# Loading a ring in single 2 MB units for three expert pairs, and a bias spread over five, in a one-core trunk kernel

## The chip, the core and the metric

The kernel runs on one core of a Trainium2 chip. The metric is device time in microseconds of one execution, the median of three runs. A profile of one further execution is at hand; its times are those of the trace.

## What is computed

One decoder layer on 256 tokens of width 1024, float32 throughout: an adaLN-conditioned token mixer (three branches, gated and projected), then an expert FFN, then a final RMSNorm. The part that matters here is the FFN. A router picks 4 of 32 experts for each token; an expert has a gate-up matrix of 1024 x 2048, a clamped SwiGLU, a down matrix of 1024 x 1024, and biases for both:

```python
def expert_block(args):
    xb, e = args
    gu = xb @ w_gu[e] + b_gu[e]
    gate, up = jnp.split(gu, 2, axis=-1)
    gate = jnp.minimum(gate, SWIGLU_LIMIT)
    up = jnp.clip(up, -SWIGLU_LIMIT, SWIGLU_LIMIT)
    glu = gate * jax.nn.sigmoid(SWIGLU_ALPHA * gate)
    return ((up + 1.0) * glu) @ w_down[e] + b_down[e]
...
y_assign = ys[dest] * w_sorted[:, None]
out = jax.ops.segment_sum(y_assign, sorted_tok, num_segments=n_tok)
```

All 32 experts' weights are read once from HBM: 403 MB of the 485 MB that the kernel moves.

## The kernel before

**Pairs.** The FFN goes through the experts in 16 pairs. For pair `p`, `gate_up(p)` multiplies the gathered tokens by eight blocks of 128 rows of both experts' gate-up matrices (`k` = 0 to 7, 2 MB each); after each block a function `during(k)` slips in other work: the gather of the next pair's tokens, block by block (`gather_k`, L1173), and after block 0 the scatter of an earlier pair's result (L1327). Then come `swiglu(p)` on VectorE and ScalarE and `down(p - 1)`, the down projections of the pair before, 4 MB for each of the two experts. So TensorE's order is gate-up 0, gate-up 1, down 0, gate-up 2, down 1 and so on. Both kinds of product are recorded at L1337 (`tiles4`); 32 of its passes belong to one gate-up block, 16 to one of the eight row blocks of a down projection.

**The ring.** Weights land in `wchunk`, a ring of seven units of 2 MB, with loads issued by SP in the order in which `add` put them on the list `loads`. `lay` assigns units: a load of size 1 takes the unit that was used longest ago, a load of size 2 an aligned couple (0 and 1, 2 and 3, or 4 and 5), so that unit 6 is left out where only such couples run. The turn of the single loads is laid so that the first couple falls on units 0 and 1. A load is issued as soon as TensorE has done the last matmul on what stood in its unit; SP waits for that, and all later loads wait behind it. A "wide" load (`add_gu2`, and a slot of size 2 in `add_dn`) is two DMAs of 2 MB, one for each expert, with rows of 16 KB, for two blocks `k`; a couple is given back by `passed` after the second of them.

**Exceptions.** `EXTRA` names blocks that are loaded singly (`add_gu`): (0, 6) in the ring, (0, 7) into free pieces of other tiles ("rest"), (1, 6) and (1, 7) into "b2" and "b4", which the mixer has left. Pair 15 and the last down projections are loaded in smaller slots; these don't change.

**The down bias.** The sum of the down biases over each token's experts is one product of the routing weights (transposed into `wT`) with the 32 rows of biases. `bias_down` does it whole, in `during(1)` of pair 7: two transposes (L1277), a copy by VectorE, and four products of 128 x 512 (L1282), each into one of the two banks of `bbank`, multiplied and added to the residual by VectorE (`add_rows`, L1268 and L1270).

Of the kernel before, what the change touches and what calls it, by code (L numbers as in the profile page):

```python
# [20 lines left out]
D = 1024  # L21
KB = D // P
T = 256
TT = T // P
FF = 1024
NE = 32
TOPK = 4
NP = NE // 2
HEADS = 8
EPS = 1e-5  # L30
SPILL = 12
LIMIT = 7.0
ALPHA = 1.702
# [43 lines left out]
def trunk(ctx: ExitStack, tc: tile.TileContext, x, c, norm1_g, ada_w, ada_b, w_in, gmlp_norm_g, gmlp_ws,  # L77
# [3 lines left out]
    V, S, G, TE = nc.vector, nc.scalar, nc.gpsimd, nc.tensor  # L81
# [28 lines left out]
    def bbank():  # L110
        return psb.tile([P, 512], F32, name="bbank")
# [8 lines left out]
    def add(fn, where=None, size=1):  # L120
        loads.append((fn, where, size))
        return len(loads) - 1
# [53 lines left out]
    def load(dst, src):  # L176
        nc.sync.dma_start(dst, src)  # L177
# [64 lines left out]
    wgu, wdn = exp_w_gu[0], exp_w_down[0]  # L242
    gu_ids, dn_ids = {}, {}


    EXTRA = {(0, KB - 2): None, (0, KB - 1): "rest", (1, KB - 2): "b2", (1, KB - 1): "b4"}

    def gu_rows(p, j):
        return wgu[2 * p:2 * p + 2, 2 * j * P:2 * (j + 1) * P, :].rearrange("e (p i) n -> p e i n", i=2)
# [11 lines left out]
    def add_gu(p, k):  # L261
        src = gu_rows(p, k // 2)[:, :, k % 2]

        def fn(t):
            c = 0
            for v in t if isinstance(t, list) else [t]:
                v = v.rearrange("p (e n) -> p e n", e=2)
                load(v, src[:, :, c:c + v.shape[2]])
                c += v.shape[2]
        gu_ids[p, k] = (add(fn, EXTRA[p, k]), None)  # L270

    def dn_rows(w, k0, k, c0, n):
        j, i = k0 // 4, k0 % 4
        v = w[4 * j * P:4 * (j + 1) * P]
        if (k, n) == (4, D):
            return v.rearrange("(p i) n -> p (i n)", i=4)
        return v[:, c0:c0 + n].rearrange("(p i) n -> p i n", i=4)[:, i:i + k]

    def add_dn(p, *slots):

        dn_ids[p] = []

        def fn(t, parts):
            off = 0
            for k0, k, c0, n in parts:
                for e in range(2):
                    v = t[:, off:off + k * n]
                    load(v if (k, n) == (4, D) else v.rearrange("p (k n) -> p k n", k=k), dn_rows(wdn[2 * p + e], k0, k, c0, n))
                    off += k * n
        for parts in slots:  # L290
            size = sum(2 * a[1] * a[3] for a in parts) // CHUNK_ELEMS
            i = add(lambda t, parts=parts: fn(t, parts), None, size)
            off = 0
            for a in parts:
                dn_ids[p].append((i, off, a is parts[-1]) + a)
                off += 2 * a[1] * a[3]

    for p in range(NP):
        for j in range(KB // 2):
            if (p, 2 * j) not in EXTRA:  # L300
                add_gu2(p, j)
            elif p == 0:
                for i in range(2):
                    add_gu(p, 2 * j + i)
            if (p, j) == (0, 1):
                for pk_ in EXTRA:
                    if pk_[0]:
                        add_gu(*pk_)
        if p:
            add_dn(p - 1, *([[(4 * j, 4, 0, D)] for j in range(2)] if p < NP - 1 else  # L310
                            [[(k, 4, c, 512)] for c in (0, 512) for k in (0, 4)]))
    add_dn(NP - 1, [(0, 4, 0, 512)], [(4, 2, 0, 512), (6, 2, 0, 512)], [(0, 4, 512, 256), (4, 4, 512, 256)],
           [(0, 4, 768, 256), (4, 2, 768, 256), (6, 2, 768, 256)])
# [25 lines left out]
    b4 = Carve(big.tile([P, CHUNK_ELEMS], F32, name="b4"))  # L339
# [92 lines left out]
    def half(h):  # L432
        return slice(h * 512, (h + 1) * 512)
# [555 lines left out]
    for o in order:  # L989
# [6 lines left out]
        name, h = o  # L996
# [38 lines left out]
    n = len(steps)  # L1035
# [94 lines left out]
    wk = {"g2b": big.tile([P, D], F32, name="x4", bufs=2)}  # L1130
# [134 lines left out]
    def add_rows(ps, tt, s, gate=False):  # L1265
        if gate:
            t = wk["su"]()
            V.tensor_tensor(t, ps, wk["g2b"][:, s], op=OP.mult)  # L1268
            ps = t
        V.tensor_tensor(xt[:, tt, s], ps, xt[:, tt, s], op=OP.add)  # L1270

    def bias_down():

        wT = wk["wT"]
        ps = bbank()
        for tt in range(TT):
            TE.transpose(ps[:NE, tt * P:(tt + 1) * P], wgt[:, tt], ident)  # L1277
        V.tensor_copy(wT, ps[:NE, :T].rearrange("p (t n) -> p t n", t=TT))
        for tt in range(TT):
            for h in range(2):  # L1280
                ps = bbank()
                TE.matmul(ps, lhsT=wT[:, tt], rhs=wk["bdn"][:, half(h)], start=True, stop=True)  # L1282
                add_rows(ps, tt, half(h), gate=True)

    def swiglu(pg, a=None):

# [69 lines left out]
    def gate_up(p, during=None):  # L1356
        sel[p] = nc.values_load(isel[0:1, p:p + 1], engines=[PE], min_val=0, max_val=1,
                                skip_runtime_bounds_check_because="one minus the result of a comparison: 0 or 1")
        pg = [abank() for _ in range(4)]
        for i, k in enumerate(in_turn(p)):  # L1360
            n, row = gu_ids[p, k]
            t = chunk(n)
            ws = []
            for v in t if isinstance(t, list) else [t]:
                v = v.rearrange("p (e n) -> p e n", e=2)
                if row is not None:
                    v = v[:, :, row * 2 * FF:(row + 1) * 2 * FF]
                ws.extend(v[:, :, c:c + 512] for c in range(0, v.shape[2], 512))
            for b in range(4):
                tiles4(pg[b], xs[p % 2][:, k], lambda e: of_expert(ws[b], e, slice(0, 512)), sel[p], i == 0, False)  # L1370
            if EXTRA.get((p, k)) is None and row != 0:
                passed(n)
            if during:
                during(i)
            if i == KB - 2:
                V.tensor_copy(ex.rearrange("p (a g) -> p a g", a=4), e2g[:, p].unsqueeze(2).to_broadcast([P, 4, GRP]))
        add_bias(pg)
        return pg
# [91 lines left out]
    for p in range(1, NP):  # L1470
        weigh(p - 1)
        if p > 1:
            turn_weights(p - 1)
            transpose_act()

        def during(k, p=p):
            if k == 0 and p >= 2:
                scatter(owT[p - 2])
            if k == 1 and p == 7:
                bias_down()  # L1480
            if p + 1 < NP:
                if k == 0:
                    one_hot(p + 1)
                else:
                    gather_k(p + 1, k - 1)
                if k == KB - 1:
                    gather_k(p + 1, k)
        pg = gate_up(p, during)
        if p == 1:
            more_work_tiles()  # L1490
            turn_weights(p - 1)
            transpose_act()
        swiglu(pg)
        if p == SPILL:
            tail = Carve(big.tile([P, CHUNK_ELEMS], F32, name="b2"))
            aT, scr1, scr2 = tail(FF).rearrange("p (k n) -> p k n", k=KB), tail(FF), tail(2 * FF)
            spills(scr2, scr1, xs[p % 2])
        if p < NP - 1:
            down(p - 1)


    p = NP - 1
# [68 lines left out]
```

## Time and profile before

| | |
|---|---|
| median of 3 runs | 1292.19 us (1291.4 to 1294.12) |
| the profiled execution | 1296.29 us |
| its span, first to last instruction | 1294.7 us |
| TensorE busy | 1217.2 us, 94% |
| VectorE, ScalarE busy | 439.9 us, 270.8 us |
| moved by DMA | 484.72 MB, 374 GB/s over the span |
| mean granted TensorE clock | 0.979 |

The mixer fills the first 340 us or so; the pairs begin at about 346. The profile cuts the span into 40 equal slices; a timeline tells what an engine ran when; the waits tell who ended an engine's idle time; and for some of the loads the trace has the time from issue to landing. A busy TensorE is not a TensorE at its peak, since matmuls are pipelined and their ends are modelled.

### The profile page before, as it was taken

What the parts mean: (1) busy time and instruction counts of PE and PEld (TensorE: products, weight loads), DVE (VectorE), ACT (ScalarE), POOL (GpSimd) and SP (SyncE); (2) the same over time, 40 slices, a digit from 0 to 9 for tenths busy, and PEclk for the clock granted to TensorE, in tenths of its full rate; (3) what the DMA queues carried; (4) which work ended last, traced back from release to release, by engine and by line L of the source; (5) the groups of instructions that cost most, each with busy time, mean ns of one, the idle gap of its engine ahead of it and who ended that gap; (6) DMA issues with size and microseconds to landing.
All of it is one profiled execution on the core that took longest, in us unless ns stands there. A gap on an engine that the chain in (4) does not pass through costs nothing. (4 is left out here: it accounts for less than half of the span.)

```text
span 1294.7 us, 22543 instructions
## 1 busy us (share of the span) xinstructions
PE 1217.2 (94%) x9653; PEld 614.1 (47%) x9654; DVE 439.9 (34%) x884; ACT 270.8 (21%) x538; POOL 11.0 (1%) x27
## 2 busy tenths in 40 slices
PE   7999999999899999898989899999989898989897
PEld 5899998999633333233333233333333333323222
DVE  3477886877431211212131223111121213121122
ACT  5564554455320000001010001000000101000011
POOL 0010000000000000000000000000000000000001
PEclk9999999999999999999999989999999999999999
DMA  9997198297798899999999989999999999999996
GB/s 342 322 386 256 49 381 296 104 390 311 258 390 360 351 427 427 427 428 428 426 426 427 427 358 429 427 426 426 427 427 427 427 427 425 420 421 427 427 389 224
DMA packets 83764, 484.72 MB, mean 374 GB/s; under 512 B 6753, under 2 KB 21161, under 8 KB 59854
## 3 DMA queue, kind: packets, MB, share of 16 engines
q1 hardware_dynamic: 82982, 481.51, 91.5%
q10 hardware_dynamic: 680, 1.71, 0.4%
q8 instruction: 80, 1.31, 0.4%
q14 instruction: 22, 0.18, 0.0%
HBM read 482.16 MB, written 1.05 MB: 373 GB/s over the span
## 5 line engine op out<-in xcount | busy, mean ns | idle before, releaser
L1337 PE MATMUL abank<-wchunk,b 128*32 (+2 forms) x4160 | 489.8, 608 | 34.9 <-DMA wchunk<-in_exp_w_down_dram 26.6
L1337 PEld LDWEIGHTS abank<-wchunk,b 128*32 128x32 f32 x4160 | 138.3, 112 | 342.4 <-issue 312.4
L1337 PE MATMUL cbank<-wchunk,b 128*32 128x512 f32 (+2 forms) x1952 | 232.5, 595 | 3.7 <-DMA wchunk<-in_exp_w_gu_dram 3.7
L1110 DVE TENSOR_SCALAR b<-bbank,a,mod 128x128 f32<-128x128 f32 x64 | 26.2, 410 | 395.9 <-PE bbank L1173 395.9
L509 DVE TENSOR_TENSOR spl<-wchunk,spl 128x512 fp32r<-128x512 f32 x196 | 132.2, 691 | 49.1 <-ACT spl L508 46.2
L1108 ACT ACTIVATE b<-bbank,mod,a 128x128 f32<-128x128 f32 x64 | 29.2, 457 | 537.9 <-PE bbank L1173 537.9
L508 ACT ACTIVATE spl<-wchunk 128x512 fp32r<-128x512 f32 x196 | 120.8, 627 | 76.3 <-PE abank L519 46.5
L516 PE MATMUL abank<-b,spl 128*128 128x256 f32 x432 | 110.3, 287 | 0.0
L1173 PEld LDWEIGHTS bbank<-spl,b 128*128 128x128 f32 x512 | 66.4, 193 | 91.4 <-issue 89.4
L517 PE MATMUL abank<-b,spl 128*128 128x256 f32 x432 | 108.3, 283 | 0.0
L1337 PEld LDWEIGHTS cbank<-wchunk,b 128*32 128x32 f32 x1952 | 55.0, 110 | 110.9 <-issue 98.1
L1173 PE MATMUL bbank<-spl,b 128*128 128x128 f32 x512 | 87.2, 300 | 1.8 <-DVE spl L1166 0.9
L516 PEld LDWEIGHTS abank<-b,spl 128*128 128x128 f32 x432 | 82.7, 191 | 3.6 <-issue 2.5
L517 PEld LDWEIGHTS abank<-b,spl 128*128 128x128 f32 x432 | 82.8, 192 | 0.2 <-issue 0.2
L1393 DVE TENSOR_TENSOR row<-abank,x 128x512 f32<-128x512 f32 (+1 forms) x32 | 21.8, 683 | 179.6 <-PE abank L1337 179.6
L1270 DVE TENSOR_TENSOR xt<-bbank,xt 128x512 f32<-128x512 f32 (+1 forms) x66 | 44.6, 675 | 107.6 <-PE bbank L1327 107.6
L519 PE MATMUL abank<-b,spl 128*128 128x256 f32 x432 | 69.7, 283 | 0.0
L1327 PE MATMUL bbank<-row,b 128*128 128x512 f32 (+1 forms) x132 | 62.7, 605 | 1.6 <-DVE row L1393 1.4
L519 PEld LDWEIGHTS abank<-b,spl 128*128 128x128 f32 x432 | 59.7, 192 | 0.0
L516 PE MATMUL cbank<-b,spl 128*128 128x256 f32 x224 | 57.2, 287 | 0.0
L517 PE MATMUL cbank<-b,spl 128*128 128x256 f32 x224 | 56.2, 283 | 0.0
L1320 ACT ACTIVATE b<-bbank 128x256 f32<-128x256 f32 x16 | 6.1, 383 | 238.5 <-PE bbank L1318 238.5
(273 smaller groups left out, 847.2 us busy)
## 6 DMA issues: line engine op xcount, KB each, us to landing
wchunk<-in_exp_w_gu_dram SPq DMA_DIRECT2D x125, 2048.0 KB, 17.3
wchunk<-in_exp_w_down_dram SPq DMA_DIRECT2D x56, 2048.0 KB, 14.6
wchunk<-in_w_in_dram SPq DMA_DIRECT2D x16, 2048.0 KB, 9.4
wchunk<-in_ada_w_dram SPq DMA_DIRECT2D x8, 2048.0 KB, 12.9
wchunk<-in_exp_w_down_dram SPq DMA_DIRECT2D x10, 1024.0 KB, 14.4
wchunk<-in_ada_w_dram SPq DMA_DIRECT2D x16, 512.0 KB, 9.5
wchunk<-in_exp_w_down_dram SPq DMA_DIRECT2D x10, 512.0 KB, 12.9
wchunk<-in_w_in_dram SPq DMA_DIRECT2D x4, 1024.0 KB, 10.5
```

Source lines behind the costliest of these rows:

```text
L508: S.activation(hi, w, AF.Copy)
L509: V.tensor_tensor(lo, w, hi.bitcast(F32), op=OP.subtract)
L516: TE.matmul(out_, lhsT=wh, rhs=xh, start=first and i == 0, stop=False)
L517: TE.matmul(out_, lhsT=wh, rhs=xl, start=False, stop=False)
L519: TE.matmul(out_, lhsT=wl, rhs=xh, start=False, stop=last_ and i == n - 1)
L1108: S.activation(out_, in_, AF.Identity, scale=a2[:, k:k + 1], bias=sh2[:, k:k + 1])
L1110: V.tensor_scalar(out_, in_, a2[:, k:k + 1], sh2[:, k:k + 1], op0=OP.mult, op1=OP.add)
L1173: TE.matmul(ps, lhsT=xn2[:, tt, k * P:(k + 1) * P], rhs=oh[p][:, tt].rearrange("p a g -> p (a g)"), start=tt == 0, stop=tt == TT - 1)
L1270: V.tensor_tensor(xt[:, tt, s], ps, xt[:, tt, s], op=OP.add)
L1327: TE.matmul(ps, lhsT=wt[:, tt * P:(tt + 1) * P], rhs=wk["yv"][:, c:c + n], start=True, stop=True)
L1337: TE.matmul(out_[g * GRP:(g + 1) * GRP], lhsT=xl[:, g * GRP:(g + 1) * GRP], rhs=w(e), start=start, stop=stop, skip_group_check=True)
L1393: V.tensor_tensor(wk["yv"][:, c:c + m], bank[c], wk["g2b"][:, c:c + m], op=OP.mult)
```

## The change

Two things. First, a constant `FINE` = 3: pairs 0 to 2 load each gate-up block singly, one DMA of 2 MB with rows of 8 KB, and the down projections of pairs 0 and 1 in four slots of one unit each (two row blocks of both experts, two DMAs of 1 MB). Wide loads begin with pair 3. (0, 6) is then no exception any more. Second, `bias_down` is cut: `turn_routing` does the transposes and the copy in pair 4, and one of the four products stands in each of pairs 5 to 8, at the same place behind the second block.

```diff
--- before.py
+++ after.py
@@ -28,6 +28,7 @@
 NP = NE // 2
 HEADS = 8
 EPS = 1e-5
+FINE = 3
 SPILL = 12
 LIMIT = 7.0
 ALPHA = 1.702
@@ -243,7 +244,7 @@
     gu_ids, dn_ids = {}, {}
 
 
-    EXTRA = {(0, KB - 2): None, (0, KB - 1): "rest", (1, KB - 2): "b2", (1, KB - 1): "b4"}
+    EXTRA = {(0, KB - 1): "rest", (1, KB - 2): "b2", (1, KB - 1): "b4"}
 
     def gu_rows(p, j):
         return wgu[2 * p:2 * p + 2, 2 * j * P:2 * (j + 1) * P, :].rearrange("e (p i) n -> p e i n", i=2)
@@ -267,13 +268,13 @@
                 v = v.rearrange("p (e n) -> p e n", e=2)
                 load(v, src[:, :, c:c + v.shape[2]])
                 c += v.shape[2]
-        gu_ids[p, k] = (add(fn, EXTRA[p, k]), None)
+        gu_ids[p, k] = (add(fn, EXTRA.get((p, k))), None)
 
     def dn_rows(w, k0, k, c0, n):
         j, i = k0 // 4, k0 % 4
         v = w[4 * j * P:4 * (j + 1) * P]
-        if (k, n) == (4, D):
-            return v.rearrange("(p i) n -> p (i n)", i=4)
+        if n == D:
+            return v.rearrange("(p i) n -> p (i n)", i=4)[:, i * D:(i + k) * D]
         return v[:, c0:c0 + n].rearrange("(p i) n -> p i n", i=4)[:, i:i + k]
 
     def add_dn(p, *slots):
@@ -285,7 +286,7 @@
             for k0, k, c0, n in parts:
                 for e in range(2):
                     v = t[:, off:off + k * n]
-                    load(v if (k, n) == (4, D) else v.rearrange("p (k n) -> p k n", k=k), dn_rows(wdn[2 * p + e], k0, k, c0, n))
+                    load(v if n == D else v.rearrange("p (k n) -> p k n", k=k), dn_rows(wdn[2 * p + e], k0, k, c0, n))
                     off += k * n
         for parts in slots:
             size = sum(2 * a[1] * a[3] for a in parts) // CHUNK_ELEMS
@@ -295,19 +296,22 @@
                 dn_ids[p].append((i, off, a is parts[-1]) + a)
                 off += 2 * a[1] * a[3]
 
+
     for p in range(NP):
         for j in range(KB // 2):
-            if (p, 2 * j) not in EXTRA:
+            if p < FINE:
+                for i in range(2):
+                    if p == 0 or (p, 2 * j + i) not in EXTRA:
+                        add_gu(p, 2 * j + i)
+            else:
                 add_gu2(p, j)
-            elif p == 0:
-                for i in range(2):
-                    add_gu(p, 2 * j + i)
             if (p, j) == (0, 1):
                 for pk_ in EXTRA:
                     if pk_[0]:
                         add_gu(*pk_)
         if p:
-            add_dn(p - 1, *([[(4 * j, 4, 0, D)] for j in range(2)] if p < NP - 1 else
+            add_dn(p - 1, *([[(4 * j, 4, 0, D)] for j in range(2)] if FINE <= p < NP - 1 else
+                            [[(2 * q, 2, 0, D)] for q in range(4)] if p < FINE else
                             [[(k, 4, c, 512)] for c in (0, 512) for k in (0, 4)]))
     add_dn(NP - 1, [(0, 4, 0, 512)], [(4, 2, 0, 512), (6, 2, 0, 512)], [(0, 4, 512, 256), (4, 4, 512, 256)],
            [(0, 4, 768, 256), (4, 2, 768, 256), (6, 2, 768, 256)])
@@ -1269,18 +1273,18 @@
             ps = t
         V.tensor_tensor(xt[:, tt, s], ps, xt[:, tt, s], op=OP.add)
 
-    def bias_down():
-
-        wT = wk["wT"]
+    def turn_routing():
+
         ps = bbank()
         for tt in range(TT):
             TE.transpose(ps[:NE, tt * P:(tt + 1) * P], wgt[:, tt], ident)
-        V.tensor_copy(wT, ps[:NE, :T].rearrange("p (t n) -> p t n", t=TT))
-        for tt in range(TT):
-            for h in range(2):
-                ps = bbank()
-                TE.matmul(ps, lhsT=wT[:, tt], rhs=wk["bdn"][:, half(h)], start=True, stop=True)
-                add_rows(ps, tt, half(h), gate=True)
+        V.tensor_copy(wk["wT"], ps[:NE, :T].rearrange("p (t n) -> p t n", t=TT))
+
+    def bias_down(tt, h):
+
+        ps = bbank()
+        TE.matmul(ps, lhsT=wk["wT"][:, tt], rhs=wk["bdn"][:, half(h)], start=True, stop=True)
+        add_rows(ps, tt, half(h), gate=True)
 
     def swiglu(pg, a=None):
 
@@ -1368,7 +1372,7 @@
                 ws.extend(v[:, :, c:c + 512] for c in range(0, v.shape[2], 512))
             for b in range(4):
                 tiles4(pg[b], xs[p % 2][:, k], lambda e: of_expert(ws[b], e, slice(0, 512)), sel[p], i == 0, False)
-            if EXTRA.get((p, k)) is None and row != 0:
+            if (p, k) not in EXTRA and row != 0:
                 passed(n)
             if during:
                 during(i)
@@ -1476,8 +1480,10 @@
         def during(k, p=p):
             if k == 0 and p >= 2:
                 scatter(owT[p - 2])
-            if k == 1 and p == 7:
-                bias_down()
+            if k == 1 and p == 4:
+                turn_routing()
+            if k == 1 and 5 <= p < 9:
+                bias_down(*divmod(p - 5, 2))
             if p + 1 < NP:
                 if k == 0:
                     one_hot(p + 1)
```

SP's loads from the first of the experts' on, before (`wchunk` is the ring, the `b` tiles are "b2", "b4" and a part of "rest", of which `spl` and `row` are the other parts; x4 is four DMAs alike):

```order
L177 DMA wchunk<-in_exp_w_gu_dram 128x4096 x4
L177 DMA b_3512<-in_exp_w_gu_dram 128x2x2048
L177 DMA b_3530<-in_exp_w_gu_dram 128x2x2048
L177 DMA wchunk<-in_exp_w_gu_dram 128x4096 x2
L177 DMA wchunk<-in_exp_w_gu_dram 128x2x2048
L177 DMA b_3798<-in_exp_w_gu_dram 128x2x1024
L177 DMA spl<-in_exp_w_gu_dram 128x2x512
L177 DMA row<-in_exp_w_gu_dram 128x2x512
L177 DMA wchunk<-in_exp_w_gu_dram 128x4096 x6
L177 DMA wchunk<-in_exp_w_down_dram 128x4096 x4
L177 DMA wchunk<-in_exp_w_gu_dram 128x4096 x8
L177 DMA wchunk<-in_exp_w_down_dram 128x4096 x4
```

and with the change:

```order
L178 DMA wchunk<-in_exp_w_gu_dram 128x2x2048 x4
L178 DMA b_3512<-in_exp_w_gu_dram 128x2x2048
L178 DMA b_3530<-in_exp_w_gu_dram 128x2x2048
L178 DMA wchunk<-in_exp_w_gu_dram 128x2x2048 x3
L178 DMA b_3798<-in_exp_w_gu_dram 128x2x1024
L178 DMA spl<-in_exp_w_gu_dram 128x2x512
L178 DMA row<-in_exp_w_gu_dram 128x2x512
L178 DMA wchunk<-in_exp_w_gu_dram 128x2x2048 x6
L178 DMA wchunk<-in_exp_w_down_dram 128x2048 x8
L178 DMA wchunk<-in_exp_w_gu_dram 128x2x2048 x8
L178 DMA wchunk<-in_exp_w_down_dram 128x2048 x8
L178 DMA wchunk<-in_exp_w_gu_dram 128x4096 x8
```

The order of the data is the same; the wide rows of 4096 elements up to the second down projection have become loads of 2 x 2048 and of 2048, and twice as many for the down projections.

TensorE in pair 7 behind the second block, before (`cbank` and `abank` are the banks of gate-up, `ident` the identity, the `b` tile of L1282 has the turned weights and the biases):

```order
L1337 ISA
L1337 MATMUL abank<-wchunk,b_3650 32x512 x4
L1277 MATMUL bbank<-ident,x_3753 32x128 x2
L1282 MATMUL bbank<-b_4281 128x512 x4
L1173 MATMUL bbank<-spl,b_3798 128x128 x2
L1337 ISA
L1337 MATMUL cbank<-wchunk,b_3650 32x512 x4
```

With the change, at that place in pair 4:

```order
L1341 ISA
L1341 MATMUL abank<-wchunk,b_3650 32x512 x4
L1280 MATMUL bbank<-ident,x_3753 32x128 x2
L1177 MATMUL bbank<-spl,b_3798 128x128 x2
L1341 ISA
L1341 MATMUL cbank<-wchunk,b_3650 32x512 x4
```

and in pair 5 (as in 6, 7 and 8):

```order
L1341 ISA
L1341 MATMUL abank<-wchunk,b_3650 32x512 x4
L1286 MATMUL bbank<-b_4286 128x512
L1177 MATMUL bbank<-spl,b_3798 128x128 x2
L1341 ISA
L1341 MATMUL cbank<-wchunk,b_3650 32x512 x4
```

The block of two transposes and four products stands in five pieces, each ahead of the gather of that block.

## Rows read from the trace of the kernel before

**Rows 1.** The page: the span, and the bytes moved in 40 equal slices of it.
```profile
span 1294.7 us, 22543 instructions
...
GB/s 342 322 386 256 49 381 296 104 390 311 258 390 360 351 427 427 427 428 428 426 426 427 427 358 429 427 426 426 427 427 427 427 427 425 420 421 427 427 389 224
```

**Rows 2.** Windows: stretch, length, busy us by engine, PEclk, DMA share, GB/s.
```profile
344.00:360.00 16.00, 15.07 (x116) 6.51 (x120) 3.41 (x6) 2.21 (x4) 0.00 (x0) 0.90 0.42 111
748.00:752.00 4.00, 4.00 (x20) 1.39 (x23) 1.75 (x4) 0.00 (x0) 0.00 (x0) 0.50 1.02 434
752.00:764.00 12.00, 12.00 (x100) 4.11 (x96) 0.41 (x1) 0.61 (x2) 0.00 (x0) 0.94 0.64 243
500.00:740.00 240.00, 221.16 (x1764) 77.94 (x1760) 46.93 (x85) 18.68 (x36) 0.00 (x0) 0.98 1.01 427
```

**Rows 3.** Waits of the DMA queue on SP: total us, times, longest.
```profile
SPq L177 <- PE abank L1337: 691.5, 77, 17.9
```

**Rows 4.** Timeline of SP: start, us, loads sent out after a wait.
```profile
356.06 0.82 SPq L177 DMA_DIRECT2D wchunk<-in_exp_w_gu_dram  x2
...
427.52 0.81 SPq L177 DMA_DIRECT2D wchunk<-in_exp_w_gu_dram  x2
...
502.89 0.80 SPq L177 DMA_DIRECT2D wchunk<-in_exp_w_gu_dram  x2
```

**Rows 5.** Two loads by tile: issue times, then us from issue to landing.
```profile
L177 SPq DMA_DIRECT2D wchunk<-in_exp_w_gu_dram x2: 328/377/426, 489.1 to 489.5; - x2
...
DMA to landing us min/median/max: 17.1/19.5/22.0
...
L177 SPq DMA_DIRECT2D b<-in_exp_w_gu_dram x1: 378/378/378, 310.8 to 310.8; - x1
...
DMA to landing us min/median/max: 8.7/8.7/8.7
```

**Rows 6.** Timeline of TensorE: start, us, work; pairs 1 to 3 around the down projection.
```profile
420.38 13.94 PE L1337 MATMUL abank<-wchunk,b 128*32 x128
...
437.12 1.92 PE L1337 MATMUL cbank<-wchunk,b 128*32 x16
...
491.79 1.92 PE L1337 MATMUL cbank<-wchunk,b 128*32 x16
...
500.93 1.90 PE L1337 MATMUL abank<-wchunk,b 128*32 x16
...
521.33 1.92 PE L1337 MATMUL cbank<-wchunk,b 128*32 x16 [1.01 <-DMA wchunk<-in_exp_w_gu_dram]
```

**Rows 7.** Timeline of TensorE in pair 7, behind its second block.
```profile
742.00 0.39 PE L1277 MATMUL bbank<-ident,x 128*32 128x128 f32 x2
742.90 3.02 PE L1282 MATMUL bbank<-b 32*128 32x512 f32 x6 [0.51 <-DVE b L1278]
...
748.82 3.64 PE L1337 MATMUL cbank<-wchunk,b 128*32 x16
```

**Rows 8.** Loads of a down projection, pairs 5, 7, 9: issue, us to landing.
```profile
L177 SPq DMA_DIRECT2D wchunk<-in_exp_w_down_dram x2: 327/379/431, 691.0 to 691.4; - x2
...
DMA to landing us min/median/max: 14.0/16.3/18.5
...
L177 SPq DMA_DIRECT2D wchunk<-in_exp_w_down_dram x2: 328/380/432, 813.7 to 814.1; - x2
...
DMA to landing us min/median/max: 13.2/15.5/17.7
...
L177 SPq DMA_DIRECT2D wchunk<-in_exp_w_down_dram x2: 328/667/1006, 931.3 to 931.7; - x2
...
DMA to landing us min/median/max: 14.3/16.7/19.1
```

**Rows 9.** Two queued loads of 1 MB near the end: issue, us to landing.
```profile
L177 SPq DMA_DIRECT2D wchunk<-in_exp_w_down_dram x2: 2562/2606/2650, 1236.8 to 1239.4; - x2
...
DMA to landing us min/median/max: 14.3/14.4/14.4
```

## Prediction

> **What bounds the kernel now.** I read the page first. The span is 1294.7 us; the line of bytes moved shows two regimes [rows 1]. From the 15th slice on (453 us) it stands at 420 to 429 GB/s until the last two, with one dent, the 24th at 358; in the slices before, it swings between 49 and 390. The stretches say the same more sharply: from 500 to 740 us the DMA engines are busy throughout at 427 GB/s while TensorE works 221 of 240 us [rows 2]. There the loads of the expert weights set the pace and TensorE waits for them. In 344 to 360 and 752 to 764 us it is the other way round: DMA share 0.42 and 0.64, TensorE busy for 15.1 of 16 and 12.0 of 12 us [rows 2]. The DMA queue's own waits say why: 691.5 us of SP's time is spent waiting for TensorE at L1337, that is, for matmuls to finish with a ring unit [rows 3]. An idle queue alone costs nothing; it costs where nothing later can make it good. So I look for the last place where the queue stood empty before an unbroken run.
>
> The end follows the queue. In steady state the first load of a down projection lands at 826.9 (813.7 plus 13.2) in one pair and at 945.6 (931.3 plus 14.3) two pairs later [rows 8]: 118.7 us for two pairs, 59.4 a pair, 4.95 us per 2 MB (a pair is 24 MB). TensorE needs less: pair 2 begins its matmuls at 437.12, pair 3 at 491.79, with no load waited for between [rows 6], so 54.7 us. TensorE has 4.7 us to spare per pair and eats up any lead.
>
> **Part 1, single units in pairs 0 to 2.** The arithmetic on TensorE stays, tile for tile. What moves is when a unit comes free. Before, a load of 4 MB needs two adjoining units, and both are given back only after the second block of the pair; the seventh unit lies idle once wide loads run. After, each 2 MB goes out as soon as one block is done, through seven units. I walked the queue with 4.95 us per unit, 1.0 us from issue to first byte (an estimate: a 2 MB load into an empty queue lands 8.7 us after issue [rows 5], 4.95 of it transfer, and the queue's restarts split the rest about 1.0 before and 2.7 behind), and TensorE's own times.
>
> First stop, in 344 to 360: the load that goes out at 356.06 [rows 4], after two blocks of pair 0, goes out one block earlier, near 350. That is 6 us of idle removed. None of this is yet a gain: TensorE gives back units at its own pace, the queue fills the ring, and stands again. In the changed kernel the next stop comes when seven units are full: pair 2's fourth block needs the first unit of pair 0's down projection. That work starts at 420.38 and takes 13.94 for 8 steps [rows 6], so two steps are done at 423.9, and bytes flow at 424.9, against 427.52 plus 1.0 before [rows 4]. From there 15 units follow (5 of pair 2's gate-up, 4 of pair 1's down, 6 of pair 3's first three wide loads); TensorE frees one every 3.5 us in a down projection (13.94 for four) and every 4.4 in a gate-up (from 502.8 to 520.3, where it begins to wait, four blocks), with one gap of 7.4 for the scatter (502.8 less 491.79 is two blocks of 3.6 and 3.9) [rows 6], so on the whole faster than the queue fills them, and the queue doesn't empty; at 424.9 + 15 x 4.95 = 499.2 it is done. Pair 3's fourth wide load now needs the units of its first, which TensorE hands back after two blocks.
>
> That hand-back is the step that decides. In the trace it is at 502.8 (row 500.93 plus 1.90), and the load goes out at 502.89 [rows 4, 6]. Up to there TensorE has waited for no load, so the time is its own and stays. What changes is what lies ahead in the queue. Before: the wide load issued at 489.1 lands its halves at 506.2 and 511.5 (issue plus 17.1 and 22.0) [rows 5], and the fourth follows behind it, 2 x 4.95 us later, at 521.4; TensorE indeed waits 1.01 us and starts on it at 521.33 [rows 6]. After: the queue is empty by 499.2, so its first half lands 8.7 us behind the issue, at 511.6, the second at 516.5. **Gain 4.9 us; I take 4.8**, and from there on all loads come that much sooner. Bounds: the gain keeps its size while the 15 units take under 79 us (5.3 each); it is nothing when they take 84 (5.6 each). Upward, if the stop of 4.7 us at 499 to 504 vanished as well, it would be 9.5.
>
> Is the lead lost again in pair 4? The same hand-back falls there at 557.6 (502.9 plus 54.7), bytes could follow at 558.6, and the queue has 12 units of work behind 503.9, until 563.3. So 4.7 us of cover, and no second stop; were TensorE 8 us later there, 3.3 of the gain would go.
>
> The halves of a down projection's load become 1 MB DMAs (eight instead of four for each of two pairs). SP's 0.4 us per issue is nothing next to 5 us of transfer. What smaller pieces cost can be read nearest at the end of the trace, where 1 MB loads with rows of 2 KB are queued: issued 1236.8 and 1239.4, landing 14.3 and 14.4 later [rows 9], so 2.7 us apart, against 2.48 for half of 4.95. At that price 8 of them add 1.8 us to the walk, which the 4.7 us stop swallows. The 2 MB singles have rows of 8 KB; the one of pair 1 that went out at 310.8 into an empty queue landed after 8.7 [rows 5], which leaves no room for a slower transfer.
>
> The Trainium skill speaks against splitting: its page SBUF — State Buffer, section The DMA setup-cost knee, asks for the largest single transfer, since each pays some 2 us whatever its size, and its page DMA: Bandwidth & Descriptors, section Measured, gives 6.15 us for 1 MB. By an estimate from the latter, 4 units at 12.3 instead of 4.95 us would add 29 us to the walk. For queued loads the trace disagrees: 2.7 us for 1 MB [rows 9].
>
> **Part 2, the bias.** Before, pair 7 holds it whole, behind its second block: two transposes at 742.00, eight matmul passes from 742.90, and the weights again only at 748.82 [rows 7]: 6.8 us, of which some 0.7 is a gather that stands there in every block. TensorE waits for VectorE in between, and in 748 to 752 its granted clock is 0.50 [rows 2], the lower of its two levels (1.2 instead of 2.4 GHz): 3.64 us for 16 passes, where 491.79 has 1.92 [rows 6, 7]. So the unit pair behind comes back late, and the queue empties at 758 us: DMA share 0.64 in 752 to 764 [rows 2]. The price at the end is best read by landings: 705.0 (691.0 plus 14.0) to 826.9 is 121.9 us over two pairs, against 118.7 undisturbed [rows 8]. **So 3.0 us** (idle time alone, 12 x 0.36 = 4.3, is the upper bound; some is made good by a quicker restart). After, pair 4 does the two transposes (0.4 us), pairs 5 to 8 one product each: about 1.0 us of TensorE (two of the eight passes) and 1.4 of VectorE, which works 47 of 240 us here [rows 2]. Behind the product stands a gather in the other of the two small banks, so no wait follows. 1.0 us against 4.7 to spare: nothing reaches the queue. I take 2.9. If each piece emptied the queue by a quarter of the old price, the term would be zero.
>
> **The sum.** 4.8 + 2.9 = 7.7 us. The profiled execution took 1296.3 us (span 1294.7), the median of the runs is 1292.2; the gain is one of queue time and holds for both: 1288.6 in a profile, **1284.5 us** as a run.
>
> **Rivals.**
> A: the bias only moves its stop (each piece a small one, by a clock that falls or a bank that isn't free). Only part 1 counts: 1292.2 - 4.8 = 1287.4. For it: one such wait did bring the clock down. Against: no VectorE result is needed by the next piece.
> B: the early lead is given back, because TensorE comes later to pair 3's hand-back (more waits on more loads) or the queue has less than 4.7 us of reserve. Only part 2 counts: 1289.3. Against: in the walk all of the first three pairs' loads land over 12 us before their use.
> C: the stop at 499 doesn't occur, as when transfers are a little slower but releases sooner: up to 9.5 + 2.9, 1279.8.
> D, slower: the finer loads transfer worse. Place: the 9 single units between 424.9 and pair 3. To undo both gains, the queue would have to reach pair 3's fourth load not at 499.2 but beyond 511.6, so from 1.4 us more per unit (6.35 instead of 4.95, 28%) on. At twice that the queue is another 12.5 us late: 1292.2 + 12.5 = 1304.7. Rows 5 and 9 show 0 and 9%. By the Trainium skill's figure above (DMA: Bandwidth & Descriptors, Measured) the walk would end at 528, some 17 us slower than before, 1309.
>
> **How the numbers follow.** Forecast 0.70, A 0.09, B 0.09, C 0.08, D 0.04. A run of this kernel can tell about 0.2% from no change, 2.6 us: the bound is 1289.6. Forecast, A and C lie clearly beyond it, B on the edge; so faster 0.87, same 0.09, slower 0.04. The range leaves out D, most of B and the far end of C: 1280.5 to 1289.0.
>
> **What would show it.** In the new profile: bytes flow again at about 350 instead of 357 us; a stop at about 419 to 425; a new one at 499 to 504, after pair 3's fourth wide load goes out at 502.9 as before and lands by 517; no TensorE wait for loads until pair 4 or later; no stop at 752 to 764, and 59.4 us per pair through pairs 5 to 8. It is wrong if the release at 502.9 moves, if the queue is still busy there, or if a stop shows up in pairs 4 to 8.

## Result and the profile after

| | before | after |
|---|---|---|
| median of 6 runs of each, on one chip | 1294.13 us (1291.4 to 1296.55) | 1287.48 us (1285.97 to 1288.33) |
| ratio of after to before | | 0.995, 95% interval 0.9936 to 0.9964 |
| the profiled execution, its span | 1296.29 us, 1294.7 us | 1285.97 us, 1284.4 us |

The changed kernel is faster by 0.5%: 6.65 us by the medians, 4.7 to 8.3 by the interval. Forecast were 7.7 us and 1284.5 us. Of the 3 us between 1284.5 and 1287.48, 1.9 come from the time before, which was 1292.19 in three runs and 1294.13 in six; the sum itself was about 1 us too large.

The page of the kernel after: the span, and the bytes moved in 40 equal slices of it (to be held against [rows 1]).

```profile
span 1284.4 us, 22566 instructions
...
GB/s 343 330 386 258 48 385 294 102 390 307 333 397 400 373 426 362 428 429 424 429 426 429 426 428 426 424 425 428 426 428 426 429 423 414 417 423 428 428 388 214
```

The dent of the 24th slice (358) is gone, and a new one has come in the 16th (362): the stop that the prediction put at 499 to 504 us. The slices ahead of it are fuller, 333 397 400 373 where 258 390 360 351 stood. Windows of the same kernel show the same places; the columns are those of [rows 2].

```profile
344.00:360.00 16.00, 15.07 (x132) 6.06 (x128) 4.90 (x13) 2.00 (x4) 0.00 (x0) 1.00 0.82 300
414.00:426.00 12.00, 12.00 (x106) 5.18 (x106) 5.47 (x9) 3.07 (x6) 0.00 (x0) 1.00 0.78 283
496.00:508.00 12.00, 12.00 (x106) 3.86 (x104) 1.84 (x4) 0.46 (x1) 0.00 (x0) 1.00 0.66 253
752.00:764.00 12.00, 10.52 (x92) 4.06 (x88) 4.06 (x7) 2.17 (x4) 0.00 (x0) 1.00 1.01 429
```

The last two columns are the DMA share and GB/s. The first stop is nearly filled (0.82 where 0.42 stood), one stands at about 420 as the walk had it, one at 500, and none at 752 to 764 any more (1.01 where 0.64 stood). Three loads that SP sends out after waits, from the timeline of the kernel after (start, us):

```profile
347.52 0.37 SPq L178 DMA_DIRECT2D wchunk<-in_exp_w_gu_dram  x1
...
421.37 0.37 SPq L178 DMA_DIRECT2D wchunk<-in_exp_w_gu_dram  x1
...
500.16 0.80 SPq L178 DMA_DIRECT2D wchunk<-in_exp_w_gu_dram  x2
```

They answer to 356.06, 427.52 and 502.89 in [rows 4]. The third is the hand-back on which the prediction rests, and was to stay where it was. It came 2.7 us earlier, but so did everything on TensorE from 347 us on, as its last rows of the mixer (L819) and its first on the experts' weights (L1337) show, of the kernel before:

```profile
339.13 1.10 PE L819 MATMUL abank<-row,ones 128*128 128x512 f32 x2
...
345.85 4.32 PE L1337 MATMUL abank<-wchunk,b 128*32 x32
```

and of the kernel after:

```profile
337.89 1.10 PE L823 MATMUL abank<-row,ones 128*128 128x512 f32 x2
...
343.82 3.64 PE L1341 MATMUL abank<-wchunk,b 128*32 x32
```

The first block ends at 350.17 in one and at 347.46 in the other. The change alters none of TensorE's work ahead of this place. Of the 2.7 us, 1.2 are there in the mixer already; the rest comes with the clock: in the profiled execution of before it was 0.90 of full speed in 344 to 360 [rows 2], after it was 1.00. The two spans, 10.3 us apart, therefore compare the change, a late mixer and a fall of the clock at once. A second execution of before without this fall (below) begins its first block at 343.61, has its span at 1292.1 and stands 7.7 us above after.

TensorE in pairs 3 to 5 of the kernel after (timeline; in brackets the idle time ahead and what ended it):

```profile
517.52 1.92 PE L1341 MATMUL cbank<-wchunk,b 128*32 x16
...
573.00 1.93 PE L1341 MATMUL cbank<-wchunk,b 128*32 x16 [0.61 <-DMA wchunk<-in_exp_w_gu_dram]
...
592.47 8.77 PE L1341 MATMUL abank<-wchunk,b 128*32 x64 [2.61 <-DMA wchunk<-in_exp_w_down_dram]
...
614.94 1.12 PE L1286 MATMUL bbank<-b 32*128 32x512 f32 x2
...
616.63 1.92 PE L1341 MATMUL cbank<-wchunk,b 128*32 x16
```

At 517.52 stands the block that waited 1.01 us at 521.33 before [rows 6]: it waits no more. The first wait on a load comes in pair 4, at 573.0. The bias product of pair 5 takes 1.12 us, no wait stands behind it, and the next block runs at 1.92 us for 16 passes, where the whole bias had left 3.64 [rows 7]. The first loads of the down projections in pairs 5 and 7 of the kernel after, by issue and time to landing:

```profile
L178 SPq DMA_DIRECT2D wchunk<-in_exp_w_down_dram x2: 328/376/423, 683.1 to 683.5; - x2
...
DMA to landing us min/median/max: 13.6/15.9/18.1
...
L178 SPq DMA_DIRECT2D wchunk<-in_exp_w_down_dram x2: 328/376/424, 803.5 to 803.9; - x2
...
DMA to landing us min/median/max: 12.2/14.4/16.7
```

They land at 696.7 and 815.7, 119.0 us apart, where [rows 8] gave 121.9. The first is 8.3 us earlier than before; 2.7 of that is the earlier start.

### The profile page after: what moved, and what is told of

It reads as the page before. It is cut to its first block, busy times and chain, and to the rows that moved or that the text cites. A ratio compares the mean times of both kernels' runs of the same rounds, so it can differ in the third digit from the quotient of the medians.

```text
span 1284.4 us, 22566 instructions
## 1 busy us (share of the span) xinstructions
PE 1201.3 (94%) x9653; PEld 610.6 (48%) x9654; DVE 439.9 (34%) x884; ACT 270.7 (21%) x538; POOL 11.0 (1%) x27
## 3 DMA queue, kind: packets, MB, share of 16 engines
HBM read 482.16 MB, written 1.05 MB: 376 GB/s over the span
## 5 line engine op out<-in xcount | busy, mean ns | idle before, releaser
L1341 PE MATMUL abank<-wchunk,b 128*32 (+2 forms) x4160 | 479.0, 597 | 37.9 <-DMA wchunk<-in_exp_w_down_dram 29.7
```

Of the source, the lines that this page charges most:

```text
L1341: TE.matmul(out_[g * GRP:(g + 1) * GRP], lhsT=xl[:, g * GRP:(g + 1) * GRP], rhs=w(e), start=start, stop=stop, skip_group_check=True)
```

## The experiments

Every kernel was timed, 5 to 12 times, beside the kernel before on the same chip. "Gain" is one minus the ratio, times the median of before there.

| kernel | single loads in pairs | bias | median us | ratio, 95% interval | gain us |
|---|---|---|---|---|---|
| after | 0 to 2 | spread | 1287.48 | 0.995 (0.9936 to 0.9964) | 6.5 |
| loads only | 0 to 2 | whole | 1288.2 | 0.9961 (0.9947 to 0.9976) | 5.0 |
| bias only | none | spread | 1292.42 | 0.999 (0.9981 to 1.0) | 1.3 |
| two pairs | 0, 1 | spread | 1290.53 | 0.9984 (0.9973 to 0.9995) | 2.1 |
| pair 2 only | 2 | spread | 1288.79 | 0.9961 (0.9946 to 0.9975) | 5.0 |
| six units | 0 to 2 | spread | 1288.65 | 0.9951 (0.9938 to 0.9965) | 6.3 |
| four pairs | 0 to 3 | spread | 1285.0 | 0.9927 (0.9913 to 0.994) | 9.4 |
| pairs 1 to 3 | 1 to 3 | spread | 1284.21 | 0.9924 (0.9908 to 0.9939) | 9.8 |
| five pairs | 0 to 4 | spread | 1285.11 | 0.9923 (0.991 to 0.9937) | 10.0 |
| fifteen, bias spread | 0 to 14 | spread | 1293.09 | 0.9993 (0.9982 to 1.0005) | 0.9 |
| fifteen, bias whole | 0 to 14 | whole | 1291.89 | 0.9985 (0.9975 to 0.9996) | 1.9 |

### The loads alone, the bias alone

The loads alone: the changed kernel with the bias whole in pair 7.

```diff
-            if k == 1 and p == 4:
+            if k == 1 and p == 7:
                 turn_routing()
-            if k == 1 and 5 <= p < 9:
-                bias_down(*divmod(p - 5, 2))
+                for q in range(4):
+                    bias_down(*divmod(q, 2))
```

> The single loads in pairs 0 to 2 alone; the bias stays whole in pair 7, as before. Hand-back theory (the gain is what the queue is ahead when it last stands empty, 4.8 us at pair 3's fourth wide load): 4.8 us faster than before, and a stop at about 750 to 760 us again. Rival 'the two parts help each other' (with the earlier lead the whole bias costs nothing): the full 6.6 us or so of the changed kernel, with no stop there.

Measured: 5.0 us (3.1 to 6.9) of gain, where 4.8 were forecast for part 1. The rival's 6.6 us lie in the interval too, and the stop that was expected again at 750 to 760 us is not in this kernel's trace: the DMA share is 1.01 in 752 to 764 us and 0.97 in 740 to 764. So the time doesn't tell the two apart; that the term stands is shown further down, by what the queue has moved ahead of pair 7.

The bias alone: the kernel before with the cut bias.

```diff
-            if k == 1 and p == 7:
-                bias_down()
+            if k == 1 and p == 4:
+                turn_routing()
+            if k == 1 and 5 <= p < 9:
+                bias_down(*divmod(p - 5, 2))
```

> The bias spread over pairs 4 to 8 alone; loads as before. Theory (the price of the stop behind the whole bias, read from landings): 2.9 us faster than before, no stop at 752 to 764 us, the stops before 450 us as before. Rival A of the prediction (each piece brings a small stop of its own): within 1 us of before.

Measured: 1.3 us (0 to 2.5); the forecast of 2.9 lies outside, and the "within 1 us" of rival A does not. The time alone therefore doesn't speak against A; the trace does. The stop in pair 7 did go, as a window of this kernel shows (the last two columns again DMA share and GB/s):

```profile
740.00:764.00 24.00, 24.00 (x210) 8.18 (x203) 1.29 (x5) 1.37 (x3) 0.00 (x0) 1.00 1.01 426
```

So the cause was removed and was worth less than one profile had said. The two parts together, 5.0 + 1.3 = 6.3, agree with 6.5 for both.

### The kernel before, twice more

No edit; each was run once for its trace, to see what of the first trace was the kernel's and what that execution's.

> The kernel before, unchanged, profiled once more: how long does the TensorE clock stay at the lower level behind the whole bias of pair 7, and how long does the DMA queue stand there? If the price of 2.9 us was the reading of one execution: the low stretch is 3.4 us instead of 6.8 and the idle time 1 us or so instead of 4. If it is a fixed price: as in the first profile.

> The same as the run before it, a third profile of the kernel before: the same question, and whether the low clock at 344 us at the start of the pairs (2.7 us later from there on) is in every execution.

Measured: 1293.7 us (span 1292.1) and 1293.56 us (span 1292.0). The window on pair 7 in the second trace of before:

```profile
740.00:764.00 24.00, 23.80 (x152) 7.74 (x152) 5.99 (x10) 0.92 (x2) 0.00 (x0) 0.86 0.81 332
```

TensorE's first block behind the bias in the same trace (cbank and abank are its two halves):

```profile
745.73 3.64 PE L1337 MATMUL cbank<-wchunk,b 128*32 x16
749.15 2.57 PE L1337 MATMUL abank<-wchunk,b 128*32 x16
```

The window on pair 7 in the third trace:

```profile
740.00:764.00 24.00, 23.09 (x162) 7.41 (x155) 6.40 (x11) 0.92 (x2) 0.00 (x0) 0.93 0.92 374
```

The first block behind the bias there:

```profile
747.00 3.50 PE L1337 MATMUL cbank<-wchunk,b 128*32 x16
750.33 1.89 PE L1337 MATMUL abank<-wchunk,b 128*32 x16
```

In the second, TensorE's clock is low into the block's second half (2.57 us for 16 passes); in the third it is back at full speed there (1.89). The queue stood still for 24 x (1 - 0.81) = 4.6 us in one and 1.9 us in the other. By landings (down loads of pairs 5 and 7, worked out as in [rows 8]) two pairs took 123.2 (700.8 to 824.0) and 120.5 us (703.6 to 824.1), and 121.9 in the first trace, against 119.0 undisturbed: a price of 4.2, 1.5 and 2.9 us for the same instructions. With the loads' part in place it was smaller still; TensorE behind the bias in the kernel with the loads alone:

```profile
739.14 2.74 PE L1341 MATMUL cbank<-wchunk,b 128*32 x16
741.71 1.89 PE L1341 MATMUL abank<-wchunk,b 128*32 x16
```

Here two pairs took 118.9 us (landings at 697.0 and 815.9): no price at all in that execution. Whether the lead covers the whole bias in every execution isn't shown.

The same three traces give a measure for part 1 that doesn't mix with the bias: the bytes moved from 340 to 600 us. The window in the first trace of before (the last column is GB/s):

```profile
340.00:600.00 260.00, 246.90 (x2018) 90.21 (x2017) 61.34 (x144) 29.17 (x57) 0.00 (x0) 0.99 0.94 386
```

In the second trace of before:

```profile
340.00:600.00 260.00, 247.34 (x2041) 89.92 (x2045) 60.05 (x138) 27.76 (x55) 0.00 (x0) 0.99 0.94 389
```

In the third trace of before:

```profile
340.00:600.00 260.00, 247.05 (x2018) 89.97 (x2017) 61.33 (x145) 29.22 (x57) 0.00 (x0) 0.99 0.94 387
```

In the trace of after:

```profile
340.00:600.00 260.00, 250.74 (x2075) 90.61 (x2079) 60.62 (x140) 27.91 (x55) 0.00 (x0) 0.99 0.97 397
```

One GB/s over 260 us is 0.6 us of a queue that runs at 427. Executions with the fall of the clock at 344 (the first and third of before) have to be held against each other, and so those without. After against the second of before: (397 - 389) x 260 / 427 = 4.9 us. That is part 1, once more.

The column is rounded to 1 GB/s. The traces' lists of DMA packets give the same without rounding and without the different starts: the time from the end of TensorE's first block of pair 0 until SP's queue has moved its 200th to 220th MB (the mean over these, some 600 to 655 us into the execution and ahead of pair 7). It is 281.5 to 281.7 us in the three traces of before and 281.6 with the bias alone, and 277.1 in after and with the loads alone: 4.5 us. Below it is called the packet time.

### Which of the pairs brings it

Two pairs: pair 2's gate-up and pair 1's down projection are wide again.

```diff
-FINE = 3
+FINE = 2
```

Pair 2 only: the rest wide, as before.

```diff
-FINE = 3
+FINE = (2,)
...
-            if p < FINE:
+            if p in FINE or (p, j) == (0, 3):
...
-            else:
+            elif (p, 2 * j) not in EXTRA:
                 add_gu2(p, j)
...
-            add_dn(p - 1, *([[(4 * j, 4, 0, D)] for j in range(2)] if FINE <= p < NP - 1 else
-                            [[(2 * q, 2, 0, D)] for q in range(4)] if p < FINE else
+            add_dn(p - 1, *([[(4 * j, 4, 0, D)] for j in range(2)] if p not in FINE and p < NP - 1 else
+                            [[(2 * q, 2, 0, D)] for q in range(4)] if p in FINE else
```

> The changed kernel with single loads in pairs 0 and 1 only. Hand-back theory: the wide loads of pair 2 then wait for couples as before, the last stop ends where it ended before, and the whole gain of the loads is gone: 2.9 us below before, from the bias alone. Rival 'grain' (a like share for each pair): two thirds of part 1 stay, 6 us below before.

> The changed kernel with pairs 0 and 1 loaded wide again and only pair 2 (with the down projection of pair 1 in it) in single units; bias spread. Hand-back theory: the idle time in pairs 0 and 1 never counted, the last stop is met by pair 2's loads alone: as fast as the changed kernel, 6.5 us below before. Rival 'grain': a third of part 1, 3 us below before.

Measured: two pairs gain 2.1 us (0.6 to 3.5), not to be told from the bias alone (1.3); by bytes, 390 against 389 GB/s in 340 to 600 us, and a packet time of 281.6 us, that of before. Pair 2 alone gains 5.0 (3.2 to 7.0), 396 GB/s, or 4.3 us; its packet time is 277.5, 4.0 us less than before. Single loads in pairs 0 and 1 gain nothing that shows by themselves, though with them the queue flows better early on. The kernel with two pairs shows why, first in a window:

```profile
428.00:452.00 24.00, 22.76 (x178) 7.89 (x174) 5.22 (x9) 2.04 (x4) 0.00 (x0) 1.00 0.64 260
```

The load that ends this stop, in SP's timeline of the same kernel:

```profile
445.83 0.80 SPq L178 DMA_DIRECT2D wchunk<-in_exp_w_gu_dram  x2
```

The idle time that was taken away at 350 comes back at 430 to 446, where the first wide couple has to come free whole: 24 x 0.36 = 8.6 us. With pair 2 alone it is the other way round. Four windows of that kernel:

```profile
344.00:360.00 16.00, 15.07 (x132) 6.05 (x136) 4.79 (x13) 2.11 (x4) 0.00 (x0) 1.00 0.51 166
380.00:396.00 16.00, 16.00 (x144) 5.46 (x136) 6.23 (x11) 3.35 (x5) 0.00 (x0) 1.00 0.68 267
420.00:432.00 12.00, 11.71 (x112) 3.33 (x104) 2.14 (x4) 0.00 (x0) 0.00 (x0) 1.00 1.01 402
496.00:508.00 12.00, 12.00 (x102) 3.85 (x104) 1.95 (x4) 0.46 (x1) 0.00 (x0) 1.00 1.00 423
```

It stands still early (0.51 and 0.68), but then not again: neither at 420 nor at 500. Less idle early and one more stop late, or more idle early and none late, come to nearly the same. How the idle time is divided doesn't matter; how far the queue has got when its last stop is over does.

### Six units or seven

The prediction said that the single loads go "through seven units". Here they go through six behind pair 0's seventh block.

```diff
-        turn = -sum(where is None for _, where, _ in loads[:first]) % RING
+        turn = -sum(where is None for _, where, _ in loads[:gu_ids[0, 0][0]]) % RING
...
-            u = min(range(0, RING - size + 1, size), key=lambda u: max(of[u:u + size]))
+            units = RING - 1 if gu_ids[0, 6][0] < i < first else RING
+            u = min(range(0, units - size + 1, size), key=lambda u: max(of[u:u + size]))
```

> The changed kernel with the single loads behind pair 0 kept to six units (the seventh left out, as wide loads leave it out). Does the gain of part 1 come from the seventh unit or from handing back single units? Theory as predicted (seven units): some of the 4.8 us goes. A walk of the queue with the same prices says that with six units the queue is still ahead at pair 3's fourth wide load, by 0.4 us less: 7 us below before. Rival 'capacity' (the seventh unit is the gain): 3 us below before, the bias alone.

Measured: 6.3 us (4.5 to 8.0), as with seven; the packet time is 277.5 us, 0.4 more than with seven. The seventh unit is not what brings the gain; giving back after one block instead of two is. (That a finer load also lands sooner brings nothing by itself ahead of the last stop: in 345 to 530 us TensorE of the kernel before waits for a load once, the 1.01 us of [rows 6].) The stops of this kernel lie elsewhere: DMA share 0.63 in 380 to 396 and 0.78 in 420 to 432, and, as with pair 2 alone, none at 500.

### Single loads further on

Four pairs, so that pair 3's first couple is given back unit by unit too and the stop at 500 should go; five pairs; and pairs 1 to 3, in the form above that takes a list.

```diff
-FINE = 3
+FINE = 4
```
```diff
-FINE = 3
+FINE = 5
```
```diff
-FINE = (2,)
+FINE = (1, 2, 3)
```

> The changed kernel with single loads in pairs 0 to 3 instead of 0 to 2. Hand-back theory: pair 3 then has no couple of units to wait for, so the stop of some 4 us at 499 to 504 goes, the queue runs on, and the time falls by a further 4.6 us, to 12 us below before in all. Rival 'grain' (each pair of finer loads saves a like share of part 1): a further 1.6 us, 9 below before. Rival 'transfer' (finer loads cost rate): no further gain or a loss.

> The changed kernel with single loads in pairs 0 to 4. Hand-back theory: the last stop is gone already with pairs 0 to 3, so the fifth pair adds nothing: 12 us below before, the same as with four. Rival 'grain': a further 1.6 us, more than with four. Rival 'transfer': less than with four.

> The changed kernel with single loads in pairs 1, 2 and 3, pair 0 wide as before; bias spread. Hand-back theory: as with pairs 0 to 3, some 9.5 us below before, since what pair 0 does is made good by TensorE's own pace. Rival 'grain': three pairs as in the changed kernel, 6.5 below before.

Measured: 9.4 (7.8 to 11.3), 10.0 (8.2 to 11.6) and 9.8 us (7.9 to 11.9), where some 12 were expected of the first. In the kernel with four pairs the stop at 500 is gone:

```profile
496.00:508.00 12.00, 12.00 (x87) 3.91 (x89) 3.51 (x6) 0.40 (x1) 0.00 (x0) 1.00 1.01 420
```

By bytes: 400 GB/s in 340 to 600 us for four pairs and for pairs 1 to 3, both with the clock's fall at 344, against 387: 7.9 us, of which the first 4.9 are the changed kernel's. The packet times are 273.4 and 273.8 us, 8.1 and 7.8 less than before. So the stop at 500, 12 x (1 - 0.66) = 4.1 us idle, gives 3 to 3.7 us when it goes. Five pairs move 397 GB/s, in an execution whose clock fell further (0.83 in 344 to 360); their packet time is 274.2. A fifth pair gives nothing, since there is no further stop, and pair 0 is not needed. The version with pairs 1 to 3, like those with four and five pairs, is faster than both kernels: each interval overlaps the changed kernel's (4.7 to 8.3), but the three agree, and the packet times with them.

### Single loads nearly to the end

If the size of a load costs nothing, this keeps the gain of four pairs. One kernel has the bias spread; the other has it whole, by the edit of the kernel with the loads alone on top.

```diff
-FINE = 3
+FINE = 15
```

> Single loads in pairs 0 to 14 with the bias spread. Hand-back theory: no different from single loads in pairs 0 to 3 or 0 to 4 (12 us below before), and the same as with the bias whole if that costs nothing here. Rival 'transfer': slower than these by 7 us for each 1% of rate.

> Single loads in pairs 0 to 14, with the bias whole in pair 7. Two questions. Do finer loads transfer slower? Theory: no, the steady pairs take 59.4 us as before; rival 'transfer': longer, each 1% being 0.6 us a pair and 7 us in all. And does the whole bias still cost its 2.9 us? A walk with seven single units says the queue has enough to do during the bias and the price is nothing: 12 us below before; theory of a fixed price: 9 below.

Measured: 0.9 (-0.6 to 2.3) and 1.9 us (0.5 to 3.2) of gain; against five pairs, 8.0 and 6.8 us slower by the medians. Here the transfers tell. The stretch 600 to 900 us, where the kernel with five pairs has wide loads only:

```profile
600.00:900.00 300.00, 278.43 (x2198) 97.60 (x2198) 63.03 (x114) 23.36 (x45) 0.00 (x0) 0.98 1.01 426
```

and the kernel with single loads to pair 14 (bias whole):

```profile
600.00:900.00 300.00, 276.84 (x2208) 94.83 (x2204) 63.89 (x114) 23.36 (x45) 0.00 (x0) 0.99 1.01 421
```

Both queues are busy throughout (1.01); the one with rows of 8 KB moves 421 GB/s, the one with rows of 16 KB 426. It is the rows and not the size of a load: a single gate-up load has 2 MB, as each half of a wide one has, and in the finer kernel gate-up loads of 2 MB (838 to 874 us) and down loads of 1 MB (878 to 896) move 421 and 420. In 860 to 1040 us it is 421 against 427 of the kernel before. For a unit of 2.097 MB that is 4.98 against 4.91 us, 1.4%, and for a pair of 12 units 0.8 us. Ten more pairs make some 8; by the packets the 200th to the 450th MB, ten pairs' worth, take 596.0 us here and 589.4 with five pairs, 6.6 more. That is most of what was lost. The queue of both kernels also stands still once more at the end, in 1210 to 1220 us, where the wide loads of pair 15 begin: DMA share 0.73 and 0.74 there, 0.97 with five pairs, some 2.4 us. No run separates the two. The whole bias makes no stop in this kernel: the DMA share is 1.01 in 736 to 760, although the granted clock is 0.97 there. The two kernels can't be told apart by their times.

## Why the prediction was right, and where it was off

**What bounds the kernel** was read rightly: queue time that is lost before the last stop counts, once, and at the size it has there. The kernel with two pairs took away idle time at 350 and gained nothing by it; the one with pair 2 alone left it there and kept most of the gain.

**Part 1, 4.8 us**: measured 5.0 as time, 4.9 by bytes and 4.5 by packet time. The steps came as put down: flow again at 347.5 (about 350 less the 2.7 us of the earlier start), a stop at 414 to 426, a new one at 496 to 508, the deciding load at the hand-back and no wait for it (517.52). Two of its reasons were wrong. "Through seven units" is not needed: six do. And that [rows 5] left "no room for a slower transfer" was read from one load into an empty queue; queued, rows of 8 KB cost 1.4%. Over the 9 single units among the 15 of the walk that is 0.6 us, well within the 4.7 us of the stop that swallowed it, so the sum didn't show it. Rival C did not occur in the changed kernel, but its price can be told from the kernel with four pairs: the stop is worth 3 to 3.7 us, not 4.7.

**Part 2, 2.9 us**: mis-sized; 1.3 us as time (0 to 2.5). The mechanism was right: a wait of TensorE for VectorE, a low clock behind it, a late hand-back, an empty queue, and none of it left when the bias is spread. But its price was read from the landings of one execution, and it rests on how long the clock stays low, which differs from one execution to the next: 4.2, 1.5 and 2.9 us in three traces, and nothing in the trace of the loads alone. Why the timed runs gave 1.3 where the mean of the three traces is 2.9 isn't settled: a timed run leaves no rows. It does leave its mean granted clock. The three traces have 0.979, 0.983 and 0.983; of 55 timed runs of the kernel before, 34 have more than 0.983, and their median is 0.985. So all three traces are of executions with more time at the lower clock than is usual, which fits a smaller price in the usual one; where in a run the clock fell isn't on record.

**The sum** was 7.7 and came out as 6.5 (4.7 to 8.3). The measured 1287.48 us is the very time that rival A gave, 1287.4, but by the way of a slower time before: A's gain was 4.8, and it lies at the edge of the interval. The spread pieces make no stop in the bias-only kernel's pair 7, and in after the DMA share over 600 to 900 us, with pairs 5 to 8 in it, is 1.01; A needs stops there. Rival B fell with 4.5 to 4.9 us still there behind 600 us. Rival D has the right sign at the wrong size: 1.4% a unit, not 28. The Trainium skill, page SBUF — State Buffer, section The DMA setup-cost knee, asks for the largest single transfer. This case's traces don't bear it out in a queue that always has work: loads of 1 MB and of 2 MB move 420 and 421 GB/s there, and what the finer kernel loses (421 against 426) goes with the rows. Ahead of the last stop the unit that comes free earlier is worth more than either. The 6.15 us for 1 MB of the Trainium skill, page DMA: Bandwidth & Descriptors, section Measured, is no price for queued loads: at 421 GB/s, 1.05 MB take 2.5 us in the queue.

## What to carry to other kernels

Find the last place where the bottleneck's queue stands still, and take away what stands behind that one; idle time ahead of it is given back. Fine loads are worth their price up to there and cost from there on, so load finely only until the ring runs without a stop, and coarsely after. A cost that hangs on a clock that rises and falls should be read from several executions, and two spans compared only after their starts have been.

## What the hardware showed unexpectedly

Rows of 8 KB move 420 to 421 GB/s from a queue that never stands, in loads of 2 MB and of 1 MB alike, and rows of 16 KB 426 to 427, on one core that runs alone.

The same program got TensorE's full clock (2.4 GHz) at 344 us in some executions and in others not: in three executions of the kernel before, 32 passes took 3.64 us in one, and 4.32 and 4.46 in the two where part of them ran at the lower level (1.2 GHz). These two were also 1.4 us late already, from the first 30 us of the execution on (at the mixer's last rows, L819, 339.13 and 339.17 against 337.69); together this moved all that follows by 2.9 us. The spans of three executions of the kernel before are 1294.7, 1292.1 and 1292.0 us: the second has the full clock at 344 and the long fall behind the bias, the third has the fall at 344 and the short one behind the bias, the first has a fall at 344 and a long one.
